# A two-layer diffusion backbone on one core: alternated value products, three-pass scores, a new order of output tiles, and side work in whole chunks

## The chip, the cores and the metric

The kernel runs on one core of a Trainium2 chip. A core has four compute engines: TensorE (PE in the profile, with its weight loads as PEld), VectorE (DVE), ScalarE (ACT) and GpSimd (POOL). SyncE (SP) issues most DMAs. Each engine works its own instruction queue in order and meets the others through semaphores. The metric is the time of one execution on the device in microseconds; lower is better. The kernel before takes 2943.49 us, the median of three runs (2942.41 to 2950.72).

## The reference

The model has two layers over 256 latent tokens, with 256 context tokens beside them that read context only. Everything is float32, and D is 1024.

```python
for l in range(2):
    h, hc = modulate(rmsnorm(x), ...), modulate(rmsnorm(ctx), ...)
    f, p, q, k, v, gates = split_proj(h @ w_in[l])        # the same for hc
    q, k = rope(rmsnorm(q)), rope(rmsnorm(k))             # 8 query heads, 2 kv heads, 64 wide
    ya = softmax(q @ k_all.T / 8) @ v_all @ attn_proj[l]  # latents read all 512 keys
    yf, yp = fourier_branch(f), pool_branch(p)
    x = x + m2 * ((g0 * yf + g1 * yp + g2 * ya) @ w_out[l])
    # the context does the same with its own 256 keys, in layer 0 only
    h2 = modulate(rmsnorm(x), ...)
    x = x + m5 * peer(h2)                                 # the context too, in layer 0 only

def peer(x):   # 8 heads choose 16 of 16384 experts for each token
    s1, i1 = top16(q1 @ keys1.T); s2, i2 = top16(q2 @ keys2.T)
    top, pos = top16(s1[:, None] + s2[None, :])           # expert = 128 * i1 + i2
    return sum(softmax(top) * gelu(u[expert] . x) * v[expert])
```

## The kernel before, in words

Matmuls that need float32 accuracy are mostly done in three passes: each operand is split into a high and a low part of the type fp32r (`split_to`, L286 to L289: ACT writes the high part, DVE or POOL subtracts it), and `mm3` (L281 to L284) adds high x high, high x low and low x high. Some smaller products and all transposes take plain float32 operands instead.

All weights come through one stream of 1 MB tiles (`Stream`, three `raw` buffers). The order of the stream is written out by hand. `split` hands out a tile's two parts and splits the next; a load goes out on SP as soon as the buffer that it takes is free, and what SP issues later waits behind it.

A layer has these stages. `mixer` projects the tokens, mixes them and multiplies by gates. Inside it is the attention stage, a software pipeline over items (head pair `hc`, query block `b`, head `e` of the pair): 32 items in layer 0 and 16 in layer 1. Item n's scores are one product of plain float32 operands with 64 contraction rows and 512 keys (256 for context blocks) as columns (L667); DVE takes the row maximum, ACT the exponential (L673), DVE divides by the sum (`stage_norm`, L678 and L679), PE transposes the probabilities (L685), ACT copies them to the ring (L687), and PE multiplies them with the values (L700), 128 x 64 x 128 for each key block of 128, into the half of a PSUM tile that belongs to head e. Between them run 24 of the 32 steps of `filler`: the first four gate projections, six three-pass matmuls a step. Eight steps run ahead of the loop. The two heads of a pair use the same key-value head.

After `mixer` the output projection makes tiles `wout(n, b)`, n for 256 output columns and b for a block of 128 tokens; blocks 0 and 1 are latents, 2 and 3 context (layer 0 only). A tile is 24 matmuls. When the four tiles of a block are done, `wout_end(b)` stores the block (L1258, on SP) and computes its row norm on ACT and DVE. `nrm.trans(0, q)` transposes the normalised latents on PE (L451), and `nrm.cols(0, q)` scales them (L472 on DVE, L474 on ACT) and splits them. `keys()` transposes the expert keys (L1229). For `peer` of layer 0 the PSUM pool is laid out anew, with six banks and one wide tile.

`peer` begins with eight query projections (L1040 to L1062), between them the products for layer 1's conditioning (`ada_item`, L333: four products of 512 columns in four 32-column groups for each megabyte tile). Then comes the u stage: 64 steps, each with 256 experts: DVE transposes a u tile in 32 x 32 blocks (`u_T`, L1011), ACT and POOL split it (L1018, L1025), and PE runs 48 matmuls (two halves `a` of 24), whose result ACT passes through gelu (L1130) and stores to DRAM as H. In layer 1 a matmul has 256 columns. The v stage multiplies with the gate matrix and accumulates the output (L1180).

Beside the projections and the u stage runs `side()`, a generator that emits side work in pieces, each with a price: ranking (`top16`), positions (`places`), and the gate matrix in chunks of 8 tokens. A chunk's call first emits the products of the chunk before (L896, L897, 16 records on PE) and their copies (L899 on ACT), and after every fourth chunk a store of 2 MB to DRAM; then it builds the one-hot tiles of its own chunk (L911, L919, L920, L924 on DVE, L923 on ACT). It yields 4.6 in layer 1, and then a `None`. `pump(budget)` adds to a debt and draws pieces while the debt is over 2.0; a `None` ends the call. In a u step of layer 1 it is called twice, after half `a == 0` and at the end, with 1.6 each and 0.6 more at the end once the chunks have begun (L1117 to L1146). After step 54 whatever is left is emitted in one go.

Of the kernel before, what the change touches and what calls it, by code (L numbers as in the profile page):

```python
# [11 lines left out]
F32R = mybir.dt.float32r  # L12
# [48 lines left out]
def kernel(ctx_: ExitStack, tc: tile.TileContext, I, C, out):  # L61
    nc = tc.nc
# [32 lines left out]
    def b8(shape, dt=F32, name="b8"):  # L95
        return b8_p.tile(shape, dt, tag="b8", name=name)

    def b4(shape, dt=F32, name="b4"):
        return b4_p.tile(shape, dt, tag="b4", name=name)
# [4 lines left out]
    def psum(shape=(128, 512), dt=F32, name="ps"):  # L104
        return banks["ps"].tile(list(shape), dt, tag="ps", name=name)
# [374 lines left out]
    def mixer(l, nrm, last):  # L480
# [78 lines left out]
                nc.vector.tensor_tensor(out=v, in0=v, in1=rope[:, b, 0:1, :].to_broadcast([128, nh, HD]), op=OP.mult)  # L559
                nc.vector.tensor_tensor(out=src, in0=src, in1=t, op=OP.add)  # L560

        kT = b4([128, 512], name="kT")
        qT = b8([128, 4, nt], name="qT")
        for b in range(4):
            rot(b, KV[:, b, :128], 8, 2)
            if b < nq:
# [73 lines left out]
                yield from gate_sums(u, lambda c, ps, n=n: nc.scalar.activation(store[:, n, c, :], ps, AF.Copy), True)  # L640

        filler = fill()
        for _ in range(8):
            next(filler)
        ps = psum()
        for b in range(4):
            nc.tensor.transpose(ps[:, b * 128:(b + 1) * 128], KV[:, b, :128], ident)
        nc.scalar.activation(kT, ps, AF.Copy)
        for j in range(4):
            ps = psum()  # L650
            for b in range(nq):
                nc.tensor.transpose(ps[:, b * 128:(b + 1) * 128], P[:, b, 512 + j * 128:640 + j * 128], ident)
            nc.scalar.activation(qT[:, j, :], ps[:, :nt], AF.Copy)

        items = [(hc, b, e) for hc in range(4) for b in range(nq) for e in range(2)]
        st = {}
        ring = b16([128, 8, 512], name="ring")

        def stage_scores(n):
            hc, b, e = items[n]  # L660
            h = 2 * hc + e
            v, j = divmod(h, 4)
            kb = (0, 4) if b < 2 else (2, 4)
            nk = (kb[1] - kb[0]) * 128
            ps = psum()
            s = slice(64 * v, 64 * v + 64)
            nc.tensor.matmul(ps[:, :nk], lhsT=qT[s, j, b * 128:(b + 1) * 128], rhs=kT[s, kb[0] * 128:kb[1] * 128],  # L667
                             start=True, stop=True)
            mx = small([128, 3], name="mx", bufs=6)
            nc.vector.tensor_reduce(out=mx[:, 0:1], in_=ps[:, :nk], op=OP.max, axis=AX)  # L670
            nc.vector.tensor_scalar(mx[:, 0:1], mx[:, 0:1], -0.125, None, op0=OP.mult)
            pm = ring[:, n % 4, :]
            nc.scalar.activation(pm[:, :nk], ps[:, :nk], AF.Exp, bias=mx[:, 0:1], scale=0.125, accum_out=mx[:, 1:2])  # L673
            st[n] = (pm, mx, kb, nk)
# [15 lines left out]
        ya = {}  # L690

        def stage_pv(n):
            hc, b, e = items[n]
            v = (2 * hc + e) // 4
            pT, kb = st.pop(n)
            if b == 0 and e == 0:
                ya[hc] = psum(name="ya")
            for q in range(kb[0], kb[1]):
                o = (q - kb[0]) * 128
                nc.tensor.matmul(ya[hc][64 * e:64 * e + 64, b * 128:(b + 1) * 128],  # L700
                                 lhsT=KV[:, q, 128 + 64 * v:192 + 64 * v], rhs=pT[:, o:o + 128],
                                 start=q == kb[0], stop=q == kb[1] - 1)
            if b == nq - 1 and e == 1:
                split_to(yh[:, 4 + hc, :], yl[:, 4 + hc, :], ya.pop(hc)[:, :nt])

        N = len(items)
# [1 line left out]
        if l:  # L708
            ffn_rows(l)
        for n in range(N + 3):  # L710
            if 0 <= n - 1 < N:
                stage_norm(n - 1)
            if n < N:
                stage_scores(n)
            while filled < min(24 * (n + 1) // N, 24):
                next(filler, None)
                filled += 1
            if 0 <= n - 2 < N:
                stage_T(n - 2)
            if n >= 3:  # L720
                stage_pv(n - 3)
        for _ in filler:
            pass
# [44 lines left out]
    def peer(l, nrm, kT, nb, fin):  # L768
# [225 lines left out]
        def pump(budget):  # L994
            debt[0] += budget
            while debt[0] > 2.0:
                c = next(sd, 0.0)
                if c is None or c == 0.0:
                    return
                if c < 0:  # L1000
                    debt[0] = 0.0
                    return
                debt[0] -= c
# [103 lines left out]

        S.pool = False
        S.depth = 1
        per, extra = (5.4, 1.2) if nb == 4 else (3.2, 0.6)  # L1110
        USTEPS = 112
        for st in range(NSTEP):
            if st + LEAD + 1 < NSTEP:
                u_T(st + LEAD + 1)
            if st + LEAD < NSTEP:
                u_hi(st + LEAD)
            t = UH.pop(st)  # L1117
            keep = st >= NSTEP - 4 * KEEP
            if not keep:
                Hg = b4([128, 2, nt], name="Hg")  # L1120
            else:
                if st % 4 == 0:
                    HK[st // 4] = b16([128, 8, nt], name="Hk")
                Hg = HK[st // 4][:, 2 * (st % 4):2 * (st % 4) + 2, :]
            for a in range(2):
                ps = psum()
                for k in range(KD):
                    mm3(ps[:, :nt], t[:, 0, a, k].rearrange("p c e -> p (c e)"), t[:, 1, a, k].rearrange("p c e -> p (c e)"),
                        h2h[:, k, :nt], h2l[:, k, :nt], k == 0, k == KD - 1)
                nc.scalar.activation(Hg[:, a, :], ps[:, :nt], AF.Gelu_apprx_tanh)  # L1130
                if a == 0:
                    pump(per / 2)
            if not keep:
                nc.scalar.dma_start(out=Hs[st // 4][:, (st % 4) * 2 * nt:(st % 4 + 1) * 2 * nt], in_=Hg.rearrange("p a t -> p (a t)"))
            if st + LEAD < NSTEP:
                u_lo(st + LEAD)
            if sparse is not None:
                if SP["ready"] and "from" not in SP:
                    SP["from"] = st
                picks(USTEPS * (st - SP["from"]) // (NSTEP - 1 - SP["from"]) if "from" in SP else 0)  # L1140
            pump(per / 2 + (extra if hot[0] else 0.0))
            if st == NSTEP - 10:
                SP["keep"].discard("single")
                SP["free"] = [f for f in SP["free"] if f[1] in SP["keep"]]
                for _ in sd:
                    pass  # L1146
            if st == NSTEP - 8:
                v_load(VORDER[0] // 4)
            if st == NSTEP - LEAD - 1:
                S.presplit()  # L1150
            if st == NSTEP - 2:
                for _ in v_gate(VORDER[0]):
                    pass
# [64 lines left out]
    for l in range(DEPTH):  # L1218
# [25 lines left out]
        def wout(n, b):  # L1244
            wh = wo[n][0].rearrange("p (k n) -> p k n", n=256)
            wl = wo[n][1].rearrange("p (k n) -> p k n", n=256)
            c = slice(n * 256, (n + 1) * 256)
            ps = psum()
            t = slice(b * 128, (b + 1) * 128)
            for k in range(KD):  # L1250
                m = mg[k // 4][:, :, k % 4, t]
                mm3(ps[:, :256], m[:, 0], m[:, 1], wh[:, k, :], wl[:, k, :], k == 0, k == KD - 1)
            tm = b1([128, 256], name="tm")
            nc.vector.tensor_tensor(out=tm, in0=ps[:, :256], in1=m2[b // 2][:, c], op=OP.mult)
            nc.vector.tensor_tensor(out=X[:, b, c], in0=X[:, b, c], in1=tm, op=OP.add)

        def wout_end(b):
            nc.sync.dma_start(out=xm[b], in_=X[:, b, :])  # L1258
            nrm.row(b // 2, b % 2)
# [5 lines left out]
                wout(n, b)  # L1265
        if nb == 4:
            wo[2] = S.split(("wout", l, 2))
            for b in range(nb):
                wout(2, b)
            wo[3] = S.split(("wout", l, 3))  # L1270
            kr = S.take(("keys", l)).rearrange("p (a d) -> p a d", d=128)
            for b in range(2):
                wout(3, b)
            wout_end(0)
            wout(3, 2)
            wout_end(1)
            S.presplit(True)
            wout(3, 3)
            kT = keys()
            for q in range(4):  # L1280
                nrm.trans(0, q)
            for b in (2, 3):
                wout_end(b)
            for q in range(4):
                nrm.cols(0, q)
        else:
            wo[2] = S.split(("wout", l, 2))
            wo[3] = S.split(("wout", l, 3))
            kr = S.take(("keys", l)).rearrange("p (a d) -> p a d", d=128)
            wout(2, 0)  # L1290
            wout(3, 0)
            wout_end(0)
            S.presplit(True)
            wout(2, 1)
            wout(3, 1)
            wout_end(1)
            kT = keys()
            for q in range(4):
                nrm.cols(0, q)
# [70 lines left out]
```

## Time and profile before

| | |
|---|---|
| median of 3 runs | 2943.49 us (2942.41 to 2950.72) |
| profiled execution, device time | 2943.76 us |
| its span, first to last instruction | 2942.0 us |
| PE, DVE, ACT, POOL busy | 94%, 73%, 47%, 44% of the span |
| mean granted TensorE clock | 0.97 |
| layer 0: attention, mixer to its end, u stage, v stage begin at | 135, 239, 619, 1275 us |
| layer 1: attention, u stage, v stage begin at | 1873, 2109, 2589 us |

All durations are from one profiled execution. Busy time of PE is not throughput: matmuls are pipelined, and a record's end is modelled, so the cost of a matmul is read from start to start. A product of plain float32 operands leaves two matmul records, one of fp32r operands leaves one; a transpose leaves one.

### The profile page before, as it was taken

Reading aid. Unit: us, or ns where it says so; the run is one execution under the profiler, and the core shown is the slowest. Engines: PE = TensorE matmul, PEld = TensorE weight load, DVE = VectorE, ACT = ScalarE, POOL = GpSimd, SP = SyncE. Lnnn points to the kernel's source line nnn. Section 1 sums busy time; section 2 is a strip of 40 time slices with the busy share of each in tenths; the row PEclk is TensorE's granted clock in tenths of the full one; section 3 lists DMA queues with packets and bytes.
Section 4 is the critical chain, followed back from the end, with each engine's and each line's share of the span. In section 5 each row is a group of like instructions: output and inputs, shape, how many; then the busy total and the mean of one; then the engine's idle time right before and its main releaser. Section 6 shows DMA issues by size and latency. Waiting matters only on the chain. (4 is left out here: it accounts for less than half of the span.)

```text
span 2942.0 us, 42776 instructions
## 1 busy us (share of the span) xinstructions
PE 2753.4 (94%) x16484; PEld 2403.8 (82%) x16484; DVE 2158.2 (73%) x3388; ACT 1375.9 (47%) x2243; POOL 1282.2 (44%) x698
## 2 busy tenths in 40 slices
PE   6999998799899999999999997998989989899999
PEld 4767786689888889988888886788989989888887
DVE  3444344899999985589999996555988778566666
ACT  3343223134489983333333334545446766544443
POOL 0110003237777778676666662102677655500000
PEclk8999998899999999999999999999999999899999
DMA  6215756558999999999999994337788898967775
GB/s 232 87 44 177 253 186 187 157 120 210 258 286 296 291 297 286 268 361 377 379 376 380 369 362 173 119 123 189 157 194 191 223 223 208 249 250 299 280 296 198
DMA packets 365580, 706.99 MB, mean 240 GB/s; under 512 B 25424, under 2 KB 265456, under 8 KB 351296
## 3 DMA queue, kind: packets, MB, share of 16 engines
q1 hardware_dynamic: 271104, 491.38, 56.0%
q0 software_dynamic: 36864, 134.23, 12.5%
q10 hardware_dynamic: 57408, 78.65, 7.9%
q8 instruction: 129, 2.11, 0.3%
q14 instruction: 75, 0.61, 0.1%
HBM read 619.18 MB, written 85.00 MB: 239 GB/s over the span
## 5 line engine op out<-in xcount | busy, mean ns | idle before, releaser
L1180 PE MATMUL acc<-hl,A 128*128 128x512 f32 x3840 | 871.2, 389 | 0.0
L1180 PEld LDWEIGHTS acc<-hl,A 128*128 128x128 f32 x3840 | 720.6, 188 | 150.1 <-ACT A L287 0.5
L1025 POOL TENSOR_TENSOR hl<-UT,hl 128x1024 fp32r<-128x1024 f32 x256 | 629.1, 2483 | 301.0 <-ACT hl L1018 298.9
L289 POOL TENSOR_TENSOR hl<-raw,hl 128x1024 fp32r<-128x1024 f32 x112 | 277.9, 2492 | 695.4 <-ACT hl L287 575.6
L287 ACT ACTIVATE hl<-raw 128x1024 fp32r<-128x1024 f32 x388 | 387.9, 1048 | 251.2 <-PE acc L1180 77.6
L289 DVE TENSOR_TENSOR hl<-raw,hl 128x1024 fp32r<-128x1024 f32 x276 | 349.8, 1299 | 133.5 <-ACT hl L287 133.2
L1011 DVE STREAM_TRANSPOSE UT<-raw 128x2048 f32<-128x2048 f32 x128 | 294.3, 2301 | 173.1 <-DMA raw<-in_peer_u_dram 115.0
L282 PE MATMUL ps<-hTh,hl 128*128 128x384 f32 (+2 forms) x1168 | 407.9, 349 | 4.2 <-ACT hl L1018 4.2
L284 PE MATMUL ps<-hTh,hl 128*128 128x384 f32 (+2 forms) x1168 | 402.0, 344 | 6.1 <-POOL hl L1025 6.1
L283 PE MATMUL ps<-hTl,hl 128*128 128x384 f32 (+2 forms) x1168 | 401.7, 344 | 3.5 <-POOL hTl L289 3.5
L284 PE MATMUL ps<-hT,hl 128*128 128x256 f32 x1152 | 333.7, 290 | 9.8 <-POOL hl L1025 9.8
L282 PE MATMUL ps<-hT,hl 128*128 128x256 f32 x1152 | 337.7, 293 | 1.6 <-ACT hl L1018 1.6
L283 PE MATMUL ps<-hT,hl 128*128 128x256 f32 x1152 | 333.3, 289 | 1.1 <-POOL hT L289 1.1
L1018 ACT ACTIVATE hl<-UT 128x1024 fp32r<-128x1024 f32 x256 | 256.6, 1051 | 140.1 <-DVE UT L1011 116.8
L287 ACT ACTIVATE A<-af 128x768 fp32r<-128x768 f32 (+1 forms) x128 | 94.4, 738 | 333.3 <-PE acc L1180 178.2
L282 PEld LDWEIGHTS ps<-hTh,hl 128*128 128x128 f32 x1168 | 224.8, 192 | 20.9 <-issue 4.9
L284 PEld LDWEIGHTS ps<-hT,hl 128*128 128x128 f32 x1152 | 228.4, 198 | 11.6 <-POOL hl L1025 11.6
L284 PEld LDWEIGHTS ps<-hTh,hl 128*128 128x128 f32 x1168 | 224.6, 192 | 12.1 <-POOL hl L1025 7.4
L283 PEld LDWEIGHTS ps<-hTl,hl 128*128 128x128 f32 x1168 | 225.1, 193 | 8.0 <-POOL hTl L289 3.7
L282 PEld LDWEIGHTS ps<-hT,hl 128*128 128x128 f32 x1152 | 229.6, 199 | 2.0 <-ACT hl L1018 2.0
L289 DVE TENSOR_TENSOR A<-af,A 128x768 fp32r<-128x768 f32 (+1 forms) x128 | 142.9, 1117 | 119.5 <-ACT A L287 119.5
L283 PEld LDWEIGHTS ps<-hT,hl 128*128 128x128 f32 x1152 | 229.0, 199 | 1.6 <-POOL hT L289 1.6
(245 smaller groups left out, 4795.8 us busy)
## 6 DMA issues: line engine op xcount, KB each, us to landing
raw<-in_peer_u_dram SPq DMA_DIRECT2D x512, 256.0 KB
raw<-in_peer_v_dram SPq DMA_DIRECT2D x128, 1024.0 KB
raw<-in_ada_w_dram SPq DMA_DIRECT2D x48, 1024.0 KB
G<-stg ACTq DMA_DIRECT2D x20, 2048.0 KB
raw<-in_w_in_dram SPq DMA_DIRECT2D x34, 1024.0 KB
Gq<-G SPq DMA_DIRECT2D x16, 1536.0 KB
H<-Hg ACTq DMA_DIRECT2D x56, 384.0 KB
Hq<-H SPq DMA_DIRECT2D x14, 1536.0 KB
```

The lines of the kernel that those rows point to most:

```text
L282: nc.tensor.matmul(ps, lhsT=lh, rhs=rh, start=first, stop=False)
L283: nc.tensor.matmul(ps, lhsT=lh, rhs=rl, start=False, stop=False)
L284: nc.tensor.matmul(ps, lhsT=ll, rhs=rh, start=False, stop=last)
L287: nc.scalar.activation(hi, src, AF.Copy)
L289: eng.tensor_tensor(out=lo, in0=src, in1=hi.bitcast(F32), op=OP.subtract)
L1011: nc.vector.transpose(t, r)
L1018: nc.scalar.activation(t[:, 0, a], v[:, a], AF.Copy)
L1025: nc.gpsimd.tensor_tensor(out=t[:, 1, a], in0=v[:, a], in1=t[:, 0, a].bitcast(F32), op=OP.subtract)
L1180: nc.tensor.matmul(acc[b][n], lhsT=a4[:, lhs, a, t], rhs=rhs[:, o:o + 512], start=f, stop=e)
```

## The change

It has five edits. (1) Scores: `kT` and `qT` become pairs of high and low parts, made by `split_to`, and the score product becomes `mm3`. Four of the eight filler steps that ran ahead of the transposes now run between them. (2) Value products: `stage_pv` runs on every second iteration, takes both heads of a pair, and alternates them for each key block. (3) In the loop an item's scores are emitted ahead of the normalisation of the item before. (4) Layer 0's output projection finishes blocks 0 and 1 first; the latents' transposes and scaling come ahead of the last tile and of the row norms of blocks 2 and 3. (5) In layer 1 `pump` is called once in a u step, at its end, with a budget of 4.4 (5.0 once the chunks have begun).

```diff
-        for _ in range(8):
+        for _ in range(4):
             next(filler)
...
-        nc.scalar.activation(kT, ps, AF.Copy)
+        kT = [b4([128, 512], F32R, name="kT") for _ in range(2)]
+        qT = [b8([128, 4, nt], F32R, name="qT") for _ in range(2)]
+        split_to(kT[0], kT[1], ps)
         for j in range(4):
...
-            nc.scalar.activation(qT[:, j, :], ps[:, :nt], AF.Copy)
+            split_to(qT[0][:, j, :], qT[1][:, j, :], ps[:, :nt])
+            next(filler)
...
-            nc.tensor.matmul(ps[:, :nk], lhsT=qT[s, j, b * 128:(b + 1) * 128], rhs=kT[s, kb[0] * 128:kb[1] * 128],
-                             start=True, stop=True)
+            qh, ql = (t[s, j, b * 128:(b + 1) * 128] for t in qT)
+            kh, kl = (t[s, kb[0] * 128:kb[1] * 128] for t in kT)
+            mm3(ps[:, :nk], qh, ql, kh, kl, True, True)
...
+            two = [st.pop(n - 1), st.pop(n)]
+            kb = two[0][1]
             for q in range(kb[0], kb[1]):
                 o = (q - kb[0]) * 128
-                nc.tensor.matmul(ya[hc][64 * e:64 * e + 64, b * 128:(b + 1) * 128],
-                                 lhsT=KV[:, q, 128 + 64 * v:192 + 64 * v], rhs=pT[:, o:o + 128],
-                                 start=q == kb[0], stop=q == kb[1] - 1)
+                for e, (pT, _) in enumerate(two):
+                    nc.tensor.matmul(ya[hc][64 * e:64 * e + 64, b * 128:(b + 1) * 128],
+                                     lhsT=KV[:, q, 128 + 64 * v:192 + 64 * v], rhs=pT[:, o:o + 128],
+                                     start=q == kb[0], stop=q == kb[1] - 1)
...
         for n in range(N + 3):
+            if n < N:
+                stage_scores(n)
             if 0 <= n - 1 < N:
                 stage_norm(n - 1)
-            if n < N:
-                stage_scores(n)
...
-            if n >= 3:
+            if n >= 3 and n % 2 == 0:
                 stage_pv(n - 3)
...
-        per, extra = (5.4, 1.2) if nb == 4 else (3.2, 0.6)
+        per, extra = (5.4, 1.2) if nb == 4 else (4.4, 0.6)
...
-                if a == 0:
+                if a == 0 and nb == 4:
                     pump(per / 2)
...
-            pump(per / 2 + (extra if hot[0] else 0.0))
+            pump((per / 2 if nb == 4 else per) + (extra if hot[0] else 0.0))
...
             wo[2] = S.split(("wout", l, 2))
-            for b in range(nb):
-                wout(2, b)
             wo[3] = S.split(("wout", l, 3))
             kr = S.take(("keys", l)).rearrange("p (a d) -> p a d", d=128)
             for b in range(2):
+                wout(2, b)
                 wout(3, b)
-            wout_end(0)
+                wout_end(b)
+            S.presplit(True)
+            wout(2, 2)
             wout(3, 2)
-            wout_end(1)
-            S.presplit(True)
-            wout(3, 3)
             kT = keys()
+            wout(2, 3)
             for q in range(4):
                 nrm.trans(0, q)
+            for q in range(4):
+                nrm.cols(0, q)
+            wout(3, 3)
             for b in (2, 3):
                 wout_end(b)
-            for q in range(4):
-                nrm.cols(0, q)
```

## Rows read from the trace of the kernel before

**Rows 1.** The page, part 1: busy us, share of the span, instructions.
```profile
PE 2753.4 (94%) x16484; PEld 2403.8 (82%) x16484; DVE 2158.2 (73%) x3388; ACT 1375.9 (47%) x2243; POOL 1282.2 (44%) x698
```
**Rows 2.** Stages: span, then PE, PEld, DVE, ACT, POOL busy, clock, DMA share, GB/s.
```profile
135.20:238.50 103.30, 102.30 (x497) 66.45 (x496) 44.50 (x131) 47.52 (x114) 15.26 (x8) 1.00 0.11 37
1873.40:1934.00 60.60, 60.48 (x368) 42.79 (x368) 27.85 (x67) 31.17 (x67) 16.09 (x7) 1.00 0.22 70
2109.00:2240.00 131.00, 114.77 (x903) 112.69 (x904) 115.88 (x217) 61.80 (x92) 106.85 (x41) 0.96 0.85 192
2240.00:2519.00 279.00, 242.74 (x2122) 239.80 (x2122) 221.47 (x154) 189.82 (x340) 166.13 (x71) 0.93 0.90 216
2519.00:2540.00 21.00, 13.88 (x114) 13.14 (x113) 16.61 (x14) 14.52 (x28) 5.47 (x3) 0.67 0.89 221
2540.00:2589.00 49.00, 49.00 (x411) 49.00 (x410) 15.95 (x12) 20.42 (x32) 31.72 (x14) 1.00 0.79 227
```
**Rows 3.** PE's timeline in layer 0's attention: start us, us, instruction, [idle before].
```profile
167.69 0.65 PE L700 MATMUL ya<-ring,KV 128*64 128x128 f32 x4
168.27 1.12 PE L667 MATMUL ps<-kT,qT 64*128 64x512 f32 x2
169.32 0.50 PE L282 MATMUL gate<-hTh,hl 128*128 128x512 f32 x1
169.66 0.39 PE L283 MATMUL gate<-hTl,hl 128*128 128x512 f32 x1
169.89 0.39 PE L284 MATMUL gate<-hTh,hl 128*128 128x512 f32 x1
...
171.34 1.09 PE L700 MATMUL ya<-ring,KV 128*64 128x128 f32 x8
172.36 0.70 PE L667 MATMUL ps<-kT,qT 64*128 64x256 f32 x2
172.99 0.66 PE L685 MATMUL ps<-ident,ring 128*128 128x128 f32 x4
```
**Rows 4.** Lines L667 and L700, counts: duration ns min/median/max, first, last start, forms.
```profile
L667 PE MATMUL ps<-kT,qT x96: 376/589/693, 135.2 to 1926.4; 64*128 64x512 f32 x64, 64*128 64x256 f32 x32
...
L700 PE MATMUL ya<-ring,KV x320: 272/273/324, 145.5 to 1933.8; 128*64 128x128 f32 x160
```
**Rows 5.** PE's timeline in layer 0's query projections: conditioning products.
```profile
495.64 1.49 PE L333 MATMUL adaps<-raw,cT 128*32 128x512 f32 x12
```
**Rows 6.** DVE's timeline ahead of layer 0's attention: a subtraction of `split_to`.
```profile
126.86 0.69 DVE L289 TENSOR_TENSOR yl<-pt,yh 128x512 fp32r<-128x512 f32 x1 [0.70 <-ACT yh L287]
```
**Rows 7.** PE's timeline between layer 0's output projection and query projections.
```profile
444.71 1.91 PE L451 MATMUL ps<-ident,xn 128*128 128x128 f32 x16
455.29 5.29 PE L333 MATMUL adaps<-raw,cT 128*32 128x512 f32 x24 [8.67 <-DVE hTf L472]
...
473.24 0.58 PE L283 MATMUL ps<-hTl,hl 128*128 128x256 f32 x1 [3.52 <-POOL hTl L289]
```
**Rows 8.** SP's timeline there: DMAs issued.
```profile
447.99 0.33 SPq L198 DMA_DIRECT2D raw<-in_ada_w_dram  x1
...
458.37 1.80 SPq L204 DMA_DIRECT2D raw<-in_peer_wq_dram  x4
```
**Rows 9.** ACT's timeline there.
```profile
465.71 2.01 ACT L287 ACTIVATE hl<-raw 128x1024 fp32r<-128x1024 f32 x2 [10.01 <-DMA raw<-in_peer_wq_dram]
```
**Rows 10.** DVE's timeline in layer 1's chunk steps: transposes of u.
```profile
2407.48 2.31 DVE L1011 STREAM_TRANSPOSE UT<-raw 128x2048 f32<-128x2048 f32 x1 [10.48 <-DMA raw<-in_peer_u_dram]
...
2413.75 2.30 DVE L1011 STREAM_TRANSPOSE UT<-raw 128x2048 f32<-128x2048 f32 x1
...
2421.63 2.30 DVE L1011 STREAM_TRANSPOSE UT<-raw 128x2048 f32<-128x2048 f32 x1
```
**Rows 11.** Waits in layer 1's u stage: waited for: us, times, longest us.
```profile
DVE UT L1011 <- DMA raw<-in_peer_u_dram: 62.6, 17, 10.5
...
PE ps L896 <- DVE ohs L924: 43.3, 13, 8.6
```

More of the change, by code (lines that the diff above doesn't have):

```diff
@@ L560, in rot @@
                 nc.vector.tensor_tensor(out=src, in0=src, in1=t, op=OP.add)
-        kT = b4([128, 512], name="kT")
-        qT = b8([128, 4, nt], name="qT")
         for b in range(4):
@@ L692, in stage_pv @@
         def stage_pv(n):
[L693 to L696, printed above, removed]
+            hc, b, _ = items[n]
+            v = 2 * hc // 4
+            if b == 0:
                 ya[hc] = psum(name="ya")
+            two = [st.pop(n - 1), st.pop(n)]
+            kb = two[0][1]
             for q in range(kb[0], kb[1]):
                 o = (q - kb[0]) * 128
-                nc.tensor.matmul(ya[hc][64 * e:64 * e + 64, b * 128:(b + 1) * 128],
-                                 lhsT=KV[:, q, 128 + 64 * v:192 + 64 * v], rhs=pT[:, o:o + 128],
-                                 start=q == kb[0], stop=q == kb[1] - 1)
-            if b == nq - 1 and e == 1:
+                for e, (pT, _) in enumerate(two):
+                    nc.tensor.matmul(ya[hc][64 * e:64 * e + 64, b * 128:(b + 1) * 128],
+                                     lhsT=KV[:, q, 128 + 64 * v:192 + 64 * v], rhs=pT[:, o:o + 128],
+                                     start=q == kb[0], stop=q == kb[1] - 1)
+            if b == nq - 1:
                 split_to(yh[:, 4 + hc, :], yl[:, 4 + hc, :], ya.pop(hc)[:, :nt])
```

## The prediction, written before the result

> **What bounds the kernel now.** I read the busy shares first, then the busy time by stage, then TensorE's timeline inside the stages that the change touches, and the waits last. TensorE (PE) is busy for 94% of the span [rows 1], so an edit pays if it takes matmul time off PE where PE has no idle time, or closes one of its gaps. The stage view tells the two apart [rows 2]. In both attention stages (135.2 to 238.5 us in layer 0, 1873.4 to 1934.0 us in layer 1) PE is busy 102.3 of 103.3 us and 60.5 of 60.6 us at full clock, VectorE (DVE) and ScalarE (ACT) under half of it: there PE alone sets the end. In the expert u stage of layer 1 (2109 to 2589 us, 64 steps) no engine is full: PE loses time in the first 431 us, with the clock at 0.93 to 0.96 and the DMA share at 0.85 to 0.90, and is gapless in the last 49 us only.
>
> **Products with the values.** In the timeline an item with four key blocks takes from 171.34 to 172.36 us, 1.02 us for 8 matmul records; one with two blocks from 167.69 to 168.27, 0.58 us for 4 [rows 3]. So a record costs 0.11 us and each group 0.14 us on top. Each 4-byte product leaves two records, so the 320 records [rows 4] are 32 items with four blocks (16 in each layer) and 16 with two: 32 x 1.02 + 16 x 0.58 = 41.9 us. The change alternates the two heads, which write different 64-column halves of one PSUM tile. Whether halves run at the same time is shown by the conditioning products: 12 records of 512 columns, in four 32-column groups in turn, take 1.49 us [rows 5], where a record of that width alone takes 0.42 (below), 5.0 us for twelve. They run four abreast, less the tail of the last. With two abreast a pair costs what one item does: 16 x 1.02 + 8 x 0.58 = 21.0 us, **20.9 us less** (12.8 in layer 0, 8.2 in layer 1). The lower end is that nothing overlaps and only 24 of the 48 groups' 0.14 us go, 3.4 us. I take 20.9: the row is of the same operand type with the same kind of column groups.
>
> The Trainium skill has a rule against this: "TensorE: Matmul & The Clock Gate", section "The mechanism" of its part on packing small matmuls, says that a weight load overlaps running matmuls only when its row group differs, and both halves here use all rows. "TensorEngine Tiling (Array Packing)", section "Key Properties", says that different tiles load and multiply in parallel. By the first the pair would gain nothing but the 3.4 us; by the second, half. The row with four groups abreast sides with the second.
>
> **Scores.** One product of 512 keys takes from 168.27 to 169.32, 1.05 us for two records; of 256 keys 0.63 us (172.36 to 172.99) [rows 3]: 0.42 us for a record of 512 columns, and 0.21 us of switching. The three passes that replace it are of the kind of the filler's matmuls, which start 0.23 us apart (169.66 to 169.89). So 3 x 0.23 + 0.21 = 0.90, 0.15 us less, for the 32 wide ones (64 records [rows 4]); the 16 narrow ones cost 3 x 0.12 + 0.21 = 0.57, 0.06 less (0.12 us is the pitch at 256 columns: 411 records in 49 gapless us [rows 2]). Sum **5.8 us less**. No row shows such passes on 64 rows; were each as slow as a record now, 0.42 us, scores would cost 32 x 0.42 + 16 x 0.21 = 16.8 us more. I stay with 0.23, the nearest row.
>
> Splitting kT and qT adds five subtractions on DVE in each layer, 0.69 us each at 512 columns [rows 6], on an engine busy 44.5 of 103 us [rows 2]; ACT keeps its five copies. The four side steps moved between the transposes cover this, 6 x 0.23 = 1.4 us each against a copy and a subtraction of about 1.3 us; uncovered it would be under 2 us for both layers. Scores ahead of the normalisation only reorders DVE: the transpose that needs the normalised row comes an iteration later. With shorter iterations PE may wait for ACT's copy ahead of the products, as it does for 0.2 to 0.6 us now in the iterations without side work; I allow 2 us. **Attention: 20.9 + 5.8 - 2 = 25 us less.** What PE does afterwards is bound by PE, so the gain stays.
>
> **Latent tiles first (layer 0).** After the last output product and 32 transposes (446.6 us) PE stands 8.67 us, until DVE has read the last transposed tile, because the next stage's PSUM layout takes those banks [rows 7]. That reading stands behind the context rows' norms. In the new order the latents' reading starts one product (24 x 0.12 = 2.9 us) before PE's end and ahead of those norms; it takes about 5 us, so PE would wait 2 instead of 8.7. Then the load of the third conditioning tile is late: on SP's queue it stays behind the stores of the context rows, which wait for the last product, and goes out at 447.99 as now [rows 8]. A megabyte takes 7.3 us there (issued 458.37, split begun at 465.71 [rows 9]), so that tile's products start at 455.3, not at 458.8: 3.5 us. The load at 458.37 waits for the first conditioning product and moves up with it, so ACT, which stands 10 us for it, is free earlier for the context's columns, for which PE waits 3.5 us at 473.24 [rows 7 to 9]. Bounds 0 and 10; I take **5 us less**.
>
> **Side work in layer 1.** From the code: a chunk is charged 4.6. Now 3.8 a step comes in two calls, so a chunk comes in 0.83 of the steps, in the first or the second call, 3 are left for a flush at step 54, and the chunks run in steps 19 to 54. Afterwards they run one a step, always at the step's end, in steps 14 to 46, with no flush; the ranking and index work ahead of them is pressed from 19.5 steps into 14.5. Piece by piece, against 131 + 279 + 21 + 49 = 480 us now [rows 2]:
> - Front: DVE is busy 115.9 us now, of it some 20 transposes of u by 2.3 [rows 10]; so 70 us of side work and 14.5 x 2.3 = 33 for u, 103 us at least, PE needing only 14.5 x 5.76 = 84. I take 110.
> - Chunk steps: DVE makes a u transpose and a chunk in 6.3 us (2407.48 to 2413.75) or, beside GpSimd, in 7.9 (2413.75 to 2421.63) [rows 10]. Steps with 0.83 chunk cost 279 / 34.5 = 8.1 us now, since PE stands 43.3 us in 13 waits for one-hots, and DVE 62.6 us for u loads [rows 11]; they are one chain: a load held up by the gate matrix's 2 MB stores stops DVE's in-order queue (10.48 us at 2407.48), and PE stands before the chunk's products though its next weights are ready. By my count of the calls about 32 of the 43 us fall on chunks made in one step's first call and used in the next one's, which need their u load 1.5 steps ahead of PE's use of it; at the step's end it is always 1. Without them the pace is 7.2, and 0.17 chunk more by about 5 us puts it at 8.0: 32.5 x 8.0 = 260.
> - Tail: 9 steps with stores of H at about 6.0 and 8 at 5.76: 100.
>
> Sum 470, **10 less**; as the loads' share is near full already, I take 8. Bounds: 25 less (pace 7.5), 15 more (pace 8.8).
>
> **Sum.** 25 + 5 + 8 = 38 from the profiled execution's 2943.76 (span 2942.0), which lies 0.3 from the median of the runs: **2906 us**.
>
> **Rivals.**
> 1. The gate stores bind: one chunk a step asks for the same bytes in fewer steps. DMA share 0.90 in these steps speaks for it, against it, that the gapless last 49 us move more, 227 GB/s, at 0.79 [rows 2]. Pace 8.4 to 8.7: u stage 5 more instead of 8 less, 2919 us. Chance 0.25.
> 2. The u stage gains its whole slack (pace 7.5): 25 less, 2889 us. For it: the runs of chunks with no load late keep 6.3 to 7.9. Chance 0.12.
> 3. The column halves do not overlap: 17.5 us of the gain go, 2923 us; should each of the 320 records also show its weight load, some 0.05 us (a third of what a group costs on top), 16 more, about 2940. Only the weight-load rule speaks for it. Chance 0.06.
> 4. Slower: DVE falls behind for good, because every chunk runs beside GpSimd and behind a late load. It decides above a pace of 9.2 us a step, where 110 + 32.5 x 9.2 + 100 = 509 us eats the other 30 us; at 9.5 the kernel takes 2953 us. The 10.48 us wait speaks for it, 7.9 beside GpSimd against. Chance 0.05.
>
> **Chances.** The forecast has 0.52; its own range is 2898 to 2914, the u stage off by 8 either way. Rivals 1 and 2 lie at 2919 and 2889; with the bounds of attention (wide scores 5 us dearer) and of the reordered stage (0 gained) on them, 2884 to 2934 leaves out no more than 2 in 10. What a measurement of this kernel can tell from no change is about 0.3%, 9 us: faster 0.90 (the forecast, 1, 2 and the first half of 3), same 0.05, slower 0.05.
>
> **What would show it.** Right: product records starting in twos, some 0.01 us apart, and an attention stage of layer 0 near 87 us, of layer 1 near 50; score records 0.23 us apart; the 8.67 us gap down to about 2, with a new wait for the conditioning load; no burst of chunks at step 54, the waits before chunk products well under 43 us. Wrong: product starts 0.11 us apart throughout, DVE over 95% busy in the chunk steps, or an attention stage in which PE waits for ACT or DVE.

## The result, and the profile after

The changed kernel takes 2917.49 us (median of 6 runs, 2912.30 to 2923.38), beside 2943.58 for the kernel before on the same chip: ratio 0.9911, 95% interval 0.9891 to 0.9930, so 26 us less. Below, a ratio always has its 95% interval in brackets. Forecast were 38 less, 2906 us; the time lies inside the range, but at the 2919 us of rival 1 and outside the forecast's own 2898 to 2914. The two profiled executions (spans 2942.0 and 2917.3 us) differ by stage, in us. Attention runs from the first score to the last value product, the next stage from there to the first product with the expert keys, a u stage from its first to its last gelu:

| stage | before | after | predicted change |
|---|---|---|---|
| attention, layer 0 and layer 1 | 103.2, 60.4 | 87.3, 51.1 | -25 |
| rest of the mixer to the first product with the keys, layer 0 | 255.4 | 249.4 | -5 |
| expert u stage, layer 0 | 654.4 | 660.2 | 0 |
| expert u stage, layer 1 | 474.9 | 476.5 | -8 |
| everything else | 1393.7 | 1392.8 | 0 |

Attention did what was forecast (-25.2). The reordered stage did too (-6.0), but in this execution the u stage behind it got longer by about as much. The u stage of layer 1 did not become shorter.

The page, part 1 (busy us, share of the span, instructions), which answers to [rows 1]:
```profile
PE 2727.0 (93%) x16532; PEld 2392.5 (82%) x16532; DVE 2155.0 (74%) x3398; ACT 1372.8 (47%) x2243; POOL 1280.3 (44%) x698
```
PE has 26 us less to do and is busy for a share of one point less: what was saved was PE's own time. Busy time by stage, in the columns of [rows 2]: both attentions, then the first 15 steps, the 32 chunk steps and the last 17 steps of layer 1's u stage:
```profile
135.46:222.80 87.34, 86.64 (x528) 61.92 (x528) 44.21 (x132) 46.55 (x112) 15.48 (x8) 1.00 0.13 44
1856.80:1907.90 51.10, 50.72 (x385) 39.69 (x384) 29.60 (x69) 30.03 (x64) 16.60 (x7) 1.00 0.26 84
2082.70:2190.60 107.90, 86.42 (x679) 83.67 (x679) 103.78 (x213) 47.76 (x71) 80.94 (x31) 0.94 0.78 182
2190.60:2459.70 269.10, 232.34 (x2045) 229.24 (x2044) 224.45 (x163) 191.56 (x352) 158.28 (x66) 0.90 0.85 209
2459.70:2564.90 105.20, 101.52 (x828) 100.55 (x826) 39.05 (x22) 44.58 (x70) 72.71 (x31) 0.98 0.98 236
```
In attention PE is still gapless (0.70 and 0.38 us idle). In the u stage the three pieces sum to 482.2 us, against 480 in [rows 2], and the chunk steps have the lowest clock of the three, 0.90.

PE's timeline in layer 0's attention, which answers to [rows 3]:
```profile
169.00 0.38 PE L282 MATMUL ps<-kT,qT 64*128 64x256 f32 x1
169.22 0.28 PE L283 MATMUL ps<-kT,qT 64*128 64x256 f32 x1
169.34 0.28 PE L284 MATMUL ps<-kT,qT 64*128 64x256 f32 x1
169.55 0.50 PE L282 MATMUL gate<-hTh,hl 128*128 128x512 f32 x1
...
173.92 1.09 PE L705 MATMUL ya<-ring,KV 128*64 128x128 f32 x16
174.95 0.38 PE L282 MATMUL ps<-kT,qT 64*128 64x256 f32 x1
...
181.85 0.50 PE L282 MATMUL ps<-kT,qT 64*128 64x512 f32 x1
182.19 0.39 PE L283 MATMUL ps<-kT,qT 64*128 64x512 f32 x1
182.42 0.39 PE L284 MATMUL ps<-kT,qT 64*128 64x512 f32 x1
182.74 0.50 PE L282 MATMUL gate<-hTh,hl 128*128 128x512 f32 x1
...
184.76 0.66 PE L705 MATMUL ya<-ring,KV 128*64 128x128 f32 x8
185.35 0.49 PE L282 MATMUL ps<-kT,qT 64*128 64x512 f32 x1
```
Sixteen records of a pair with four blocks go from 173.92 to 174.95, 1.03 us, as long as eight did; a pair with two blocks takes 0.59. Six of the 24 pairs take longer, as this one, which takes 1.98 us because its second head's products stand for ACT's copy of the probabilities:
```profile
167.02 0.43 PE L705 MATMUL ya<-ring,KV 128*64 128x128 f32 x2
167.98 1.09 PE L705 MATMUL ya<-ring,KV 128*64 128x128 f32 x14 [0.53 <-ACT ring L689]
```
A wide score takes from 181.85 to 182.74, 0.89 us, a narrow one 0.55.

PE's timeline between layer 0's output projection and query projections, which answers to [rows 7], and then SP's there, which answers to [rows 8]:
```profile
433.20 2.94 PE L333 MATMUL adaps<-raw,cT 128*32 128x512 f32 x16 [2.19 <-ACT junk L434]
440.58 1.93 PE L333 MATMUL adaps<-raw,cT 128*32 128x512 f32 x8 [4.44 <-DMA raw<-in_ada_w_dram]
```
```profile
425.84 8.06 SPq L1263 DMA_DIRECT2D xm<-X  x2
433.95 0.43 SPq L198 DMA_DIRECT2D raw<-in_ada_w_dram  x1
```
The gap of 8.67 us is 2.19. It does not end with the reading of the latents, which is over at 431.37, 0.4 us after PE's last product, but with ACT's first norm of the context rows (L434), and DVE reads the last output tile until 433.10, just before PE goes on:
```profile
432.68 0.42 DVE L1259 TENSOR_TENSOR tm<-ps,mrow 128x256 f32<-128x256 f32 x1
```
Behind the gap stands a wait of 4.44 for the third conditioning tile, whose load went out at 433.95, behind the stores of the context rows.

Waits in layer 1's u stage, which answer to [rows 11]:
```profile
DVE UT L1016 <- DMA raw<-in_peer_u_dram: 96.6, 22, 10.5
...
PE ps L901 <- DVE ohs L929: 36.6, 7, 6.0
```
The waits of PE for one-hots have become fewer, 7 for 13, but longer, and their sum fell by 7 us only; DVE waits 34 us more for u loads. Where these lie is shown by ACT's issue of one gate store, and by DVE's late transposes of u over the chunk steps:
```profile
2291.47 0.38 ACTq L906 DMA_DIRECT2D G<-stg  x1
```
```profile
2237.69 2.31 DVE L1016 STREAM_TRANSPOSE UT<-raw 128x2048 f32<-128x2048 f32 x1 [5.53 <-DMA raw<-in_peer_u_dram]
2273.31 2.31 DVE L1016 STREAM_TRANSPOSE UT<-raw 128x2048 f32<-128x2048 f32 x1 [6.52 <-DMA raw<-in_peer_u_dram]
2307.57 2.31 DVE L1016 STREAM_TRANSPOSE UT<-raw 128x2048 f32<-128x2048 f32 x1 [5.80 <-DMA raw<-in_peer_u_dram]
2342.28 2.31 DVE L1016 STREAM_TRANSPOSE UT<-raw 128x2048 f32<-128x2048 f32 x1 [6.30 <-issue]
...
2374.44 2.31 DVE L1016 STREAM_TRANSPOSE UT<-raw 128x2048 f32<-128x2048 f32 x1 [3.84 <-DMA raw<-in_peer_u_dram]
2409.93 2.31 DVE L1016 STREAM_TRANSPOSE UT<-raw 128x2048 f32<-128x2048 f32 x1 [6.47 <-DMA raw<-in_peer_u_dram]
2444.10 2.31 DVE L1016 STREAM_TRANSPOSE UT<-raw 128x2048 f32<-128x2048 f32 x1 [5.74 <-DMA raw<-in_peer_u_dram]
```
The late transposes come 32 to 36 us apart, every four steps (the profile names no load for the one at 2342.28), and a store of four chunks' gates is issued every four steps, 8 in the stage. PE pays for each a little later:
```profile
2313.98 0.29 PE L901 MATMUL ps<-ohs 128*128 128x128 f16 x1 [5.28 <-DVE ohs L929]
```
In two stretches of 5 us after the store at 2291.47 (columns of [rows 2]):
```profile
2296.00:2301.00 5.00, 5.00 (x45) 5.00 (x43) 4.90 (x4) 4.64 (x9) 4.45 (x3) 1.00 1.00 355
2301.00:2306.00 5.00, 5.00 (x51) 4.89 (x50) 0.77 (x1) 3.37 (x5) 4.50 (x2) 1.00 0.57 174
```
For 5 us the DMA engines are full at 355 GB/s. By the trace's packets some 1.4 MB of what they move then is of ACT's queue, which has the stores, and 0.3 MB of the queue that has the u loads; in the next 5 us DVE, with no u tile to transpose, falls from 4.90 to 0.77 us busy.

The clock is the second part of the price. In the chunk steps it is at half for 52 us. There are seven stretches at half, 48 us together, of which each begins during one of PE's seven waits for one-hots and lasts beyond it; the rest is the end of an earlier one. At half a matmul of 256 columns starts 0.21 us after the one before, for 0.12 at the full clock.

### The profile page after: what moved, and what is told of

Read it like the earlier page. It is cut to its first block, busy times and chain, and to the rows that moved or that the text cites. A ratio compares the mean times of both kernels' runs of the same rounds, so it can differ in the third digit from the quotient of the medians.

```text
span 2917.3 us, 42880 instructions
## 1 busy us (share of the span) xinstructions
PE 2727.0 (93%) x16532; PEld 2392.5 (82%) x16532; DVE 2155.0 (74%) x3398; ACT 1372.8 (47%) x2243; POOL 1280.3 (44%) x698
```

## The experiments

My theory after the result: attention gave what it gave, and the call of the side work was never the cause of the waits; the 2 MB stores are, however the chunks are called. Rivals: the late first call was a cause, and the single call's gain is hidden by something else; or the parts disturb each other.

**The parts by themselves.** Edits (1) to (3) alone, on the kernel before:
```diff
-            if n >= 3:
+            if n >= 3 and n % 2 == 0:
```
(with the scores, the pairs and the order of the loop as in the change.)

> The kernel before with the attention edits alone (three-pass scores, alternated value products, scores ahead of the normalisation). Theory: TensorE alone bounds both attention stages and what follows them, so their 25.2 us (15.9 in layer 0, 9.3 in layer 1) reach the end whole: ratio 0.9914, near 2918 us, and the other four edits together are worth nothing measurable. Rival: the later stages, bound by DMA, take some of it back; then 5 to 10 us are lost by the end, ratio 0.994 to 0.995.

Measured 2909.51 us, ratio 0.9877 [0.9861, 0.9894]: 35 us less, more than the whole change. Its attentions take 87.4 and 51.1 us, as after. The other 9 us are mostly in the u stage of layer 1, which is not edited: it takes 468.1 us with the same instructions that took 474.9. The whole stage, before and with these edits, in the columns of [rows 2]:
```profile
2114.20:2589.10 474.90, 418.13 (x3534) 412.58 (x3534) 364.71 (x394) 281.50 (x487) 305.90 (x125) 0.94 0.88 211
2087.20:2555.30 468.10, 413.68 (x3535) 408.04 (x3535) 362.14 (x394) 280.79 (x487) 305.84 (x125) 0.94 0.89 214
```
PE is idle for 54.4 us instead of 56.8 and busy for 4.5 us less, and the clock is at half for 52.5 us instead of 59.6.

Edit (4) alone:
```diff
-            for b in range(nb):
-                wout(2, b)
...
+                wout(2, b)
                 wout(3, b)
```
(with the rest of the order as in the change.)

> The kernel before with the new order of the output tiles in layer 0 alone. Theory: TensorE's 8.67 us gap falls to about 2 and the query projections begin 6 us earlier, but layer 0's u stage, whose DMA share is 0.99, ends no more than 0 to 2 us earlier: ratio 0.999 to 1.000. Rival: the 6 us reach the end, ratio 0.998, and the 6 us that layer 0's u stage was longer in the changed kernel's profile are the scatter of one execution.

Measured 2939.30, ratio 0.9982 [0.9970, 0.9994], 5 us less, as the rival had it. By the profile it is not the rival's reason: layer 0's u stage is 3 us longer (657.4 for 654.4), and the u stage of layer 1 is again shorter, 468.8.

Edit (5) alone:
```diff
-        per, extra = (5.4, 1.2) if nb == 4 else (3.2, 0.6)
+        per, extra = (5.4, 1.2) if nb == 4 else (4.4, 0.6)
...
-                if a == 0:
+                if a == 0 and nb == 4:
```

> The kernel before with the single call of side work a step in layer 1 alone. Theory: the u stage of layer 1 takes about 480 us as before, since one wait of some 6 us for a u load comes with each 2 MB store, eight of them, where there were 13 waits of 43 us before: ratio 0.999 to 1.001. Rival: the single call by itself shortens the stage by 8 us as forecast, ratio 0.997, and the other edits spoil it.

Measured 2938.62, ratio 0.9983 [0.9969, 0.9996], 5 us less, between the theory and its rival. Chunk steps and waits, in the columns of [rows 2] and [rows 11]:
```profile
2218.20:2478.70 260.50, 229.95 (x2044) 226.40 (x2043) 221.60 (x163) 192.43 (x352) 156.28 (x66) 0.93 0.88 218
```
```profile
PE ps L896 <- DVE ohs L924: 30.3, 8, 6.1
```
The pace is 260.5 / 32 = 8.14, with few and long waits as after, 8 of up to 6.1 us. Alone the three parts sum to 45 us less; together they give 26.

The changed kernel without edit (5):
```diff
-        per, extra = (5.4, 1.2) if nb == 4 else (4.4, 0.6)
+        per, extra = (5.4, 1.2) if nb == 4 else (3.2, 0.6)
```
(and the first call restored.)

> Attention edits and the new tile order, side work as before. Attention alone gave 2909.5 us, the tile order alone 5 us, all edits together 2917.5. Theory: in all these kernels layer 1's u stage takes 468 to 477 us by the way its waits for loads fall on the clock's drops to half, and nothing in the edits adds up or cancels there; then this lies at 2907 to 2918, and its u stage of layer 0 is 4 us longer than with the attention edits alone (the 5.5 us of the tile order given back). Rival: the tile order and attention edits add up, 2904.

Measured 2908.03, ratio 0.9873 [0.9854, 0.9893].

The changed kernel without edit (4), that is edits (1) to (3) and (5); the diff is that of the first run and of the third together.

> Attention edits and the single call of side work, tile order as before. Theory: the stores of 2 MB once in four steps set layer 1's u stage with the single call, 468 to 477 us; 2908 to 2918 us, so the single call is worth nothing on top of the attention edits or costs up to 8 us. Rival: the changed kernel loses 8 us against the attention edits alone through the tile order, and this kernel has 2904.

Measured 2918.5, ratio 0.9923 [0.9907, 0.9939]. So once the attention edits are in, the single call makes the kernel slower, not faster: by some 13 us without edit (4) (0.9923 against 0.9877) and by 11 with it (0.9911 against 0.9873), in ratios of 2943 us. Edit (4) is worth 1 to 3.5 us there, which these intervals do not tell from nothing.

**The stores.** The changed kernel, with each gate store of layer 1 cut into four of 512 KB, one issued with each of the following chunks:
```diff
-                        nc.scalar.dma_start(out=Gs[:, :, pc // 4, :].rearrange("g p f -> p g f"),
-                                            in_=stg.rearrange("p (g i) t -> p g (i t)", g=16))
...
+                            late += [lambda g0=g0, store=store: store(g0, 4) for g0 in range(0, 16, 4)]
+                            late.pop(0)()
```
(`store(g0, 4)` stores four of the 16 groups; the other three pieces go out at the head of the next three chunks, those of the last store together.)

> The changed kernel with each 2 MB store of layer 1's gate matrix cut into four of 512 KB (by group of the matrix, the same 1 KB runs), one for each of the next four chunks. If the burst is what costs, because u loads stand still while 2 MB pass, TensorE's eight waits of 5 to 6 us before chunk products shrink and the u stage of layer 1 falls by 20 to 40 us: near 2890 us. Rival: the DMA engines are full over the stage as a whole, the same bytes take the same time, and the waits are only spread: within 5 us of 2917.

Measured 2899.98, ratio 0.9849 [0.9833, 0.9866], some 18 us less than the changed kernel; the profiled execution, at 2895.36, lies 24 us below the changed kernel's. Its chunk steps, and PE's waits for one-hots over the u stage:
```profile
2189.50:2435.30 245.80, 226.67 (x2046) 222.61 (x2045) 213.46 (x163) 191.44 (x353) 151.80 (x65) 0.96 0.87 227
```
```profile
PE ps L904 <- DVE ohs L942: 18.7, 13, 2.6
```
The same bytes move in fewer microseconds. The pace is 7.68, the longest wait 2.6 us where it was 6.0, and the clock 0.96 where it was 0.90. The two rows account for the gain: 17.9 us of waits and 5.7 us of PE's busy time, 23.6, against 23.3 that the chunk steps became shorter. The clock is at half for 22 us of them, for 52 after the change.

The changed kernel with no gate store in layer 1 at all:
```diff
-                    if pc % 4 == 3:
+                    if pc % 4 == 3 and nb == 4:
...
-            load(out=g, in_=Gs[q])
+            load(out=g, in_=Gs[q][:, :ntg])
```
(The v stage of layer 1 reads layer 0's gate matrix in its place, as many bytes as before.)

> The changed kernel with no store of layer 1's gate matrix (the v stage of layer 1 reads layer 0's matrix in its place, so the second layer's experts are weighted wrongly). Theory: the stores' bytes and bursts are what holds the u loads up; without them the waits before chunk products go to near 0, chunk steps fall from 8.4 to about 7.4 us (a u transpose and a chunk on VectorE), the u stage from 476 to about 445, with the clock at full. If cutting the stores in four (454 us) took away only the burst, 5 to 10 us are left here for their bytes. Rival: VectorE's order and not the stores makes the waits: above 465.

Measured 2874.86 (two runs), ratio 0.9765 [0.9742, 0.9788].
```profile
2197.90:2423.80 225.90, 219.29 (x2051) 215.38 (x2050) 212.71 (x163) 191.65 (x352) 151.87 (x65) 0.99 0.81 183
```
```profile
PE ps L905 <- DVE ohs L933: 6.4, 13, 1.4
```
The pace is 7.06. Of the 43.2 us that the chunk steps lose against the changed kernel's, 30.2 are waits for one-hots and 13.0 PE's busy time at the higher clock; the clock is at half for only 4 us of the chunk steps here. So the stores cost about 43 us, and cutting them saves about half of that. Whether the other half is their bytes or the smaller bursts, no run tells apart.

**Is the single call better once the stores are cut?** The kernel with layer 1's stores cut, with two calls instead of one:
```diff
-        per, extra = (5.4, 1.2) if nb == 4 else (4.4, 0.6)
+        per, extra = (5.4, 1.2) if nb == 4 else (3.2, 0.6)
...
-                if a == 0 and nb == 4:
+                if a == 0:
```

> Attention edits, new tile order, the stores of layer 1's gate matrix cut in four as in e4, but the side work in two calls a step as before. Theory: with the bursts gone the two forms of side work differ little; the single call had its whole handicap (9 us, e5 against the changed kernel) from the regular 6 us wait at each store. So near 2895, u stage of layer 1 450 to 460 us. Rival: the two calls keep their own waits (chunks made and used in first calls, and the flush) and stay near 465, 2905 us; then the single call is the better one once the stores are cut.

Measured 2898.07, ratio 0.9843 [0.9823, 0.9864].
```profile
PE ps L904 <- DVE ohs L942: 33.6, 12, 5.4
```
Two calls still leave longer waits for one-hots (33.6 us against 18.7), as the rival had it, yet the time is the same. Then the stores of both layers cut, with two calls and with one:
```diff
-                        if nb == 2:
+                        if True:
```

> As e9, with the stores of layer 0's gate matrix cut in four as well. Layer 0's u stage has a DMA share of 0.99, and the same bytes pass: theory, no change there (within 5 us of e9). Rival: a burst stops its u loads too, twelve times, and 10 to 40 us go.

> The changed kernel (one call a step) with the stores of both layers cut in four. With the theory of e10, within 5 us of e4 (2900); with its rival 10 to 40 us less.

Measured 2899.3, ratio 0.9846 [0.9830, 0.9861], and 2896.4, ratio 0.9844 [0.9829, 0.9859]. The latter's chunk steps, then the waits with two calls and with one:
```profile
2188.70:2430.80 242.10, 222.40 (x2045) 216.94 (x2044) 214.45 (x163) 190.80 (x353) 152.89 (x66) 0.98 0.86 231
```
```profile
PE ps L904 <- DVE ohs L942: 29.8, 10, 5.9
PE ps L904 <- DVE ohs L942: 19.3, 22, 1.9
```
All four kernels with cut stores lie within 4 us of each other, less than their intervals: in the time of the program no difference shows between one call and two, and cutting layer 0's stores as well gives nothing that shows. They beat the kernel before by 1.5 to 1.6% and the changed one by 0.6 to 0.7%.

The stage itself speaks for the single call, though. In both pairs it has 10 to 15 us less of waits, and in the profiled executions the u stage of layer 1 is 5 us shorter (454.0 for 458.9) and 7 (449.2 for 456.1), where two executions of the changed kernel differ by 3. The times of the program scatter too much to show or to exclude that. So my theory is half right: beside the attention edits and with whole stores the single call makes nothing better, and a long wait comes with every store; with cut stores it does take waits away.

**Do the column halves need to alternate?** The changed kernel with a pair's heads one after the other:
```diff
-            for q in range(kb[0], kb[1]):
-                o = (q - kb[0]) * 128
-                for e, (pT, _) in enumerate(two):
+            for e, (pT, _) in enumerate(two):
+                for q in range(kb[0], kb[1]):
+                    o = (q - kb[0]) * 128
```

> The changed kernel with the two heads of a pair one after the other in the same call: all key blocks of head 0, then all of head 1, the same instructions in another order. Theory: only neighbouring products of different column halves run at the same time, so nearly all overlap goes (one product at the seam stays) and attention is longer by 16 x 0.88 + 8 x 0.44 = 17.6 us, layer 0 by 10.6 and layer 1 by 7.0. Rival: the gain came from fewer switches between tile shapes, and attention stays at 87.3 and 51.1 us.

One run, 2927.48 us. A pair in PE's timeline of layer 0's attention:
```profile
175.17 1.58 PE L705 MATMUL ya<-ring,KV 128*64 128x128 f32 x16
176.68 0.38 PE L282 MATMUL ps<-kT,qT 64*128 64x256 f32 x1
```
It takes 1.51 us: half-way between 1.03 with alternation and the 2.04 of two separate items. By the starts in the trace the first five records and the last five come about 0.11 us apart, the eight from the fifth to the twelfth within 0.38 us. A pair with two blocks, four records a head, loses nothing:
```profile
157.42 0.67 PE L705 MATMUL ya<-ring,KV 128*64 128x128 f32 x8
158.02 0.50 PE L282 MATMUL ps<-kT,qT 64*128 64x512 f32 x1
```
It takes 0.60 us, as with alternation, and its records start in twos. The attentions take 90.7 and 53.9 us, 6.2 more than after, neither the 17.6 of no overlap nor nothing. The rest of the 10 us over the changed kernel is not told from the scatter of single executions.

**The changed kernel once more:**

> The changed kernel once more, for a second profile. Theory: layer 1's u stage scatters by several us between executions of one program, and with it the time at half clock in that stage, by some 0.5 us for each us at half clock; layer 0's u stage is 656 to 664 us again, since that goes with the tile order and not with the execution. Rival: both are as in the first profile to 1 us (476.5 and 660.2 us), and differences of 8 us between kernels are theirs alone.

2914.56 us, with 654.1 us in layer 0's u stage (660.2 in the first profile) and 479.6 in layer 1's (476.5). The chunk steps:
```profile
2183.40:2452.60 269.20, 231.54 (x2045) 228.33 (x2044) 224.68 (x163) 191.33 (x352) 157.29 (x66) 0.91 0.85 210
```
269.2 us again, and a clock of 0.91: the pace of the chunk steps repeats. Layer 0's u stage does not; it scatters by 6 us between executions of one program, and the 656 to 664 us that the theory asked for did not come.

## Why the prediction was right or wrong

**Products with the values: right.** Where nothing is waited for, in 18 of the 24 pairs, a pair takes 1.03 and 0.59 us; 1.02 and 0.58 were taken. Rival 3 falls. What "TensorE: Matmul & The Clock Gate" of the Trainium skill says in "The mechanism", that a weight load overlaps running matmuls only when its row group differs, does not hold here: both halves use all rows, and a pair takes as long as one head did. "TensorEngine Tiling (Array Packing)" of the Trainium skill says in "Key Properties" that different tiles load and multiply in parallel; the trace agrees, with 1.03 us for a pair and 1.02 for one head before. With four key blocks the order matters, as the heads in turn show: 1.51 us.

**Scores: right.** 0.89 and 0.55 us for the forecast 0.90 and 0.57. By these rows products and scores are worth 27 us, and the stages became 25.2 shorter. The waits for ACT, for which 2 us were allowed, came and cost more: in the six other pairs the second head starts late, after ACT's copy, and these take 3.3 us more in all. PE's idle time does not show most of it (1.1 us in both stages, as before), since a record's modelled end covers the gap. Against it the transposes between them take 1.6 us less, from start to start, which was not forecast. So the total of 25 is met in part by luck.

**Latent tiles first: right in its place, mostly not at the end.** The gap closed to 2.19 us against "about 2", and the forecast wait for the third conditioning tile is there. The size of the gap is luck: the reading of the latents, which was to end it, is over after 0.4 us, and the rest is spent on the context's norm and the last tile's reading. 6.0 us went in the stage, 5 were forecast; over ten profiles with the edit the stage takes 250.6 us on average, over four without it 255.2. What failed, if anything, is the silent assumption that what follows would keep its length. Over the same ten profiles layer 0's u stage takes 657 us on average (653 to 664; two of them with layer 0's stores cut), over the four without it 654 (653 to 655). A stretch of that stage after the change, in the columns of [rows 2]:
```profile
740.00:1100.00 360.00, 333.92 (x2196) 300.38 (x2195) 327.66 (x319) 289.10 (x604) 272.48 (x172) 0.98 1.00 287
```
For these 360 us the DMA engines are full, so an earlier start need not end anything earlier. That fits, but the scatter is larger than the difference, and it isn't shown.

**Side work in layer 1: wrong.** The front (107.9 us for 110) and the tail (105.2 for 100) are near. The step that failed is "Without them the pace is 7.2, and 0.17 chunk more by about 5 us puts it at 8.0". It measured 269.1 / 32 = 8.41. I had counted 32 of the 43 us of waits as made by chunks that the first call emits and the next step uses. The chain was right up to its cause: a late u load stops DVE, and PE stands for the one-hots. But a chunk a step at the step's end still meets a store of 2 MB every four steps, and DVE then stands some 6 us for a u load. The waits became 7 of 5 us instead of 13 of 3. The gain that was counted on is there only once the stores are cut: then one call has 10 to 15 us less of waits than two. Rival 1 said that the stores bind, with a pace of 8.4 to 8.7. It had the place and the price, though not the whole manner: the DMA share is 0.85, and with the same bytes in pieces the pace is 7.68, so much of the price is the burst's and not the bytes'. Rival 2's pace of 7.5 is nearly reached with cut stores (7.68, and 242.1 / 32 = 7.57) and passed without any (7.06). Rival 4's pace of 9.2 was not reached.

**How the numbers followed.** 25.2 and 6.0 less, about 6 given back in layer 0's u stage in that execution, 2 more in layer 1's, and 1 less elsewhere: 24.7 between the spans, against 38. The runs of the parts give another sum: 35 to 36 less by the attention edits, 1 to 3.5 more by the tile order, 11 to 13 lost again by the single call. So edit (5), beside the others, moved the time the other way than forecast, and the total lies in the range because the bounds had room for rival 1, and because the attention edits brought 10 us more than forecast, for a reason that stays open: luck.

**What stays open.** Why the u stage of layer 1, with unchanged code in it, takes 468 us behind the attention edits or the new tile order, where the profiled execution before had 475; and so why the parts give 45 us alone and 26 together, and why the single call gains 5 us alone and costs 11 to 13 beside the attention edits. The clock has a large part in it. In the kernel before, with the attention edits alone and with the tile order alone PE is idle for 56.8, 54.4 and 56.0 us of that stage, but the clock is at half for 59.6, 52.5 and 53.1, and PE is busy for 4.5 and 5.4 us less than before. The chunk steps of the changed kernel and of edit (5) alone are the same instructions with the same stores; of the 8.6 us between them PE is idle for 6.2 and busy for 2.4, and the clock is at half for 52 and for 38 us. These are single executions. What decides how many waits bring a stretch at half clock, and how long the waits are, no run tells.

## What to carry to other kernels

When PE waits for an engine that waits for a load, look for the burst of another queue that passes just then: moving the work between calls moved the wait here, and cutting the burst into pieces spread over the consumer's steps took a good part of it away (18 us for the same bytes). Two rows of small products that use different column halves of the array should be emitted alternately: with eight records a head one head after the other cost half of the overlap, with four nothing. The gain in the stages that PE bounds was kept. Whether one ahead of a stage full of transfers is given back there was not shown; still, name that stage in the sum.

## What the runs showed of the hardware that was not expected

- Column halves overlap even without alternation: with four records a head in full (0.60 us in turn, 0.59 alternated), with eight by half (1.51 us in turn, 1.03 alternated, 2.04 for two separate items). So products of the second head start beside those of the first that were emitted ahead of them.
- Around a 2 MB store on ACT's queue the DMA engines are full (share 1.00 at 355 GB/s for 5 us), some four fifths of it the bytes of ACT's queue, and DVE stands up to 6.5 us for a u load of SP's queue. With pieces of 512 KB the longest wait that PE has for one-hots is 2.6 us.
- Waits cost more than their length. From the chunk steps without gate stores to those with them PE waits 30.2 us more, its clock falls from 0.99 to 0.90, with stretches at half that begin during the waits, and it is busy 13.0 us longer with the same matmuls.
